# A hybrid attention, RWKV and expert layer on one core: three more row buffers for the first gathers, and a scheduling priority for block 0

## The chip, the core and the metric

The kernel runs on one core of one Trainium2 chip. The engines named below are TensorE (PE, with its weight loads as PEld), VectorE (DVE), ScalarE (ACT), GpSimd (POOL) and SyncE (SP, which here only issues DMAs). The metric is the device time of one execution in microseconds. The kernel before took a median of 1790.33 us in 3 runs (1789.28 to 1791.99).

## The reference

One layer on 512 tokens of width 1024, in float32: a norm, one input projection, two groups of heads beside each other (8 latent-attention heads, 8 RWKV-7 heads), an output projection, and a retrieval over 16,384 single-neuron experts. Cut to what matters here:

```python
x = x + concat(mla_group(p_a), rwkv7_group(p_b)) @ w_o
h = rms_norm(x)                                   # 128 tokens a block, 4 blocks
s = einsum('thpd,hpnd->thpn', h @ w_pq, sub_keys)
s1, i1 = top_k(s[:, :, 0], 16); s2, i2 = top_k(s[:, :, 1], 16)
top_s, pos = top_k(s1[..., :, None] + s2[..., None, :], 16)
idx = take(i1 * 128 + i2, pos)                    # 8 heads x 16 experts a token
gate = softmax(top_s)
act = gelu(einsum('thkd,td->thk', expert_u[idx], h))
x = x + einsum('thk,thkd->td', gate * act, expert_v[idx])
```

Each token needs 128 rows of `expert_u` and 128 rows of `expert_v`, each row 1024 floats.

## The kernel before

The 512 tokens are 4 blocks of 128. The front part runs as five "lanes" of generators that a planner at the end of `layer_kernel` (from L1178) interleaves: F (norm and RWKV input projections), R (RWKV chunk products), M (latent attention), S (RWKV scan) and B (`back`: output projection, norm, retrieval, routing). B runs for block 0, then for blocks 1 and 2 together, then for block 3. I write M(2) for lane M of block 2, and so on.

Within one lane of one block the steps depend on each other. R's products (`products`, L660) are eight 64-column matmuls by 64-row halves for each level of a block inverse, masked on DVE at L674 and copied on ACT at L681; they stand in a `tc.high_priority(offset=URGENT)` block. M ends in four transposes at L518 and copies to the tile `yT` at L520. `back` begins with `out_proj` (L784 matmuls, L788 adds), then `retrieve` (L840, L847), `top16` on DVE (L819 to L827), and `route` (L854 to L959). For blocks 0 and 3 `route` ends in `idx` (L952), the row numbers of the experts.

Experts are applied in two ways. Blocks 1 and 2 (`DENSE`) go through `dense()`: for each of 128 groups of 128 experts, `up(e)` multiplies with the transposed table (L1095, or split into three products at L1109) and `down(e)` with `expert_v` (L1130, or split at L1141). The splits are made on ACT (L1055) and DVE (L1056: tiles `xl`, `ul`, `t`). `gate_half` (L1035) builds the gates. Blocks 0 and 3 (`GATHERED`) go through `experts()`: for each of the 128 experts of a token, POOL issues an indirect DMA that fetches one row per token into a tile `ga` (L970), and DVE either takes the product with the hidden state (L980, a row of `expert_u`) or adds the row to the accumulator (L983, a row of `expert_v`). Rows of u come in four groups of 32; from the second group on, each u row is followed by a v row of the group before. In all there are 512 gathers, 256 for a block. The tiles `ga` rotate through 4 buffers (`GA`): a gather can be issued only when the DVE instruction that read the fourth one back is done.

The program is recorded through a scheduling layer. It assigns each instruction a place in its engine's queue by a priority (by default the order in which it was recorded) and by its own estimate of when inputs and buffers are ready; `high_priority(offset=4000)` moves the instructions recorded in it 4000 places ahead. What comes out is a fixed order on each engine, and each engine then runs its queue strictly in that order. `experts()` is recorded after `dense()`, so its gathers have the lowest priority, and fill in from the time when `idx` is known. The pools of the early stages (`early`, L102) are closed before `dense()`, which reuses their space.

Of the kernel before, what the change touches and what calls it, by code (L numbers as in the profile page):

```python
# [2 lines left out]

# [5 lines left out]
F32 = mybir.dt.float32  # L9
# [9 lines left out]
P = 128  # L19
D = 1024  # L20
# [8 lines left out]
LNX_EPS = 64e-5  # L29
TOPK = 16  # L30
URGENT = 4000
NEG = -3.0e38
MASKED = -1.0e30
LD = -0.5 * math.exp(-0.5)
# [31 lines left out]
GATHERED = (0, 3)  # L66
DENSE = (1, 2)
EARLY = 1
GROUP, GA = 32, 4


HALF, SUB, GBUFS = 64, 16, 5
FIRST, AHEAD, KEPT = 12, 16, 12
# [14 lines left out]
def layer_kernel(ctx: ExitStack, tc: tile.TileContext, x, pos, cvec, rvec, w_mla, w_rwkv, w_uq, w_ukv, lora, g2,  # L88
# [12 lines left out]
    psums[2] = ctx.enter_context(tc.tile_pool(name="psm", bufs=1, space=PSUM))  # L101
    early = ctx.enter_context(ExitStack())  # L102
    psa = early.enter_context(tc.tile_pool(name="psa", bufs=1, space=PSUM))
    pre = early.enter_context(tc.tile_pool(name="pre", bufs=1))
    wa = early.enter_context(tc.tile_pool(name="wa", bufs=1))
    for n in (1, 4):
# [747 lines left out]
    def route(b, tv, ti):  # L854
# [103 lines left out]
        for j, dst in enumerate(slots):  # L958
            act(dst[:, o:o + P], p[:, j * P:(j + 1) * P], AF.Copy)  # L959

    def experts(b, idx, gate):
        acc = gb([P, D], "acc")
        nc.sync.dma_start(acc, x2d[b])
        h2 = gb([P, D], "h2")
        nc.sync.dma_start(h2, h2r[b])
        dots = gb([P, H * TOPK], "dots")

        def row_of(table, j):
            t = gb([P, D], "ga", GA)
            G.indirect_dma_start(out=t, out_offset=None, in_=table,  # L970
                                 in_offset=bass.IndirectOffsetOnAxis(ap=idx[:, j:j + 1], axis=0))
            return t

        ng = H * TOPK // GROUP
        for g in range(ng + 1):
            for i in range(GROUP):
                if g < ng:
                    j = g * GROUP + i
                    u = row_of(expert_u, j)
                    V.scalar_tensor_tensor(u, u, 1.0, h2, op0=OP.mult, op1=OP.mult, accum_out=dots[:, j:j + 1])  # L980
                if g:
                    j = (g - 1) * GROUP + i
                    V.scalar_tensor_tensor(acc, row_of(expert_v, j), dots[:, j:j + 1], acc, op0=OP.mult, op1=OP.add)  # L983
            if g < ng:
                sl = slice(g * GROUP, (g + 1) * GROUP)
                act(dots[:, sl], dots[:, sl], AF.Gelu)
                V.tensor_tensor(dots[:, sl], dots[:, sl], gate[:, sl], op=OP.mult)
        nc.sync.dma_start(out[b * P:(b + 1) * P, :], acc)

    state = {"carry": None}  # L990
    hTs, yTs, parts, routed = {}, {}, {}, {}
# [197 lines left out]
    while any(lanes):  # L1189
        best = None  # L1190
        for i, todo in enumerate(lanes):
            if not todo:
                continue
            t = at[i]
            if running[i] is None:
                deps = [d for b in todo[0][1] for d in after[todo[0][0]](b) if d[1] >= 0]
                if any(d not in done for d in deps):
                    continue
                t = max([t] + [done[d] for d in deps])
            if best is None or t < best[0]:  # L1200
                best = (t, i)
        t, i = best
        n, bs = lanes[i][0]
        fn, count, cost = stages[n]
        if running[i] is None:
            running[i] = fn(bs) if n == "B" else fn(*bs)
            at[i] = t
        lane[0] = LANE[n]
        try:
            next(running[i])  # L1210
            at[i] += cost / count
        except StopIteration:
            for b in bs:
                done[n, b] = at[i]
            lanes[i].pop(0)
            running[i] = None
    early.close()
    dense()
    for b in GATHERED:
        experts(b, *routed[b])  # L1220


def pack(inputs):
# [55 lines left out]
```

## Time and profile before

| | before |
|---|---|
| median of 3 runs | 1790.33 us |
| the profiled execution | 1786.83 us |
| its span, first to last instruction | 1784.9 us |
| PE busy | 1622.3 us (91%) |
| DVE busy | 1352.8 us (76%) |
| ACT busy | 907.3 us (51%) |
| POOL busy | 723.1 us (41%) |
| data moved by the indirect DMAs | 268.47 MB of 520.84 MB |

The busy time of an engine is what its instructions took, added up without overlap; it is an average over stages that have different limits. The profile gives the same numbers for any stretch of the span, and with them the clock granted to TensorE and what the DMA engines moved. "Waited for" lines name who ended an idle stretch of an engine.

### The profile page before, as it was taken

The page shows a single profiled execution, that of the slowest core. Times are in us where ns is not written, and L with a number is a line of the kernel's source. Part 1 is how long each engine was busy: PE and PEld are TensorE (multiplying, and loading weights), DVE is VectorE, ACT ScalarE, POOL GpSimd, SP SyncE. Part 2 cuts the span into 40 slices and gives each one's busy share as a digit, 9 for nine tenths or more (in the row PEclk, how much of TensorE's full clock was granted, in tenths as well). Part 3 has the DMA queues.
Part 4 walks back from the last instruction along what each step waited for, and adds up shares of the span by engine and source line. Part 5 has one row for each costly group of instructions (what it writes and reads, how often), then busy time and mean ns, then how long its engine had stood idle before and what let it go on. Part 6 is the DMA issues. An engine that isn't in the chain of part 4 may idle for free. (4 is left out here: it accounts for less than half of the span.)

```text
span 1784.9 us, 31084 instructions
## 1 busy us (share of the span) xinstructions
PE 1622.3 (91%) x11143; PEld 1363.3 (76%) x11143; DVE 1352.8 (76%) x3010; ACT 907.3 (51%) x2421; POOL 723.1 (41%) x560
## 2 busy tenths in 40 slices
PE   7999998998879995789997799999989889999998
PEld 6896898877665784667995478888867778888876
DVE  3422446667775698987889789999878799999895
ACT  5645635444422622257766234444777735444444
POOL 1001100447664433555445343544555554447430
PEclk9999997995769998998998999999989999999999
DMA  8545643898789998889997799999889889999985
GB/s 276 187 139 191 237 163 111 322 313 268 262 272 329 318 313 305 287 297 331 376 328 244 284 363 355 330 348 340 313 318 324 310 306 355 373 340 333 354 280 177
DMA packets 154875, 520.84 MB, mean 292 GB/s; under 512 B 17313, under 2 KB 24097, under 8 KB 154721
## 3 DMA queue, kind: packets, MB, share of 16 engines
q0 software_dynamic: 73728, 268.47, 43.1%
q1 hardware_dynamic: 80992, 250.39, 39.3%
q8 instruction: 88, 1.44, 0.3%
q14 instruction: 67, 0.54, 0.1%
HBM read 508.96 MB, written 9.83 MB: 291 GB/s over the span
## 5 line engine op out<-in xcount | busy, mean ns | idle before, releaser
L970 POOL DMA_INDIRECT ga<-in_expert_v_dram,idx x256 | 359.0, 1402 | 366.7 <-DVE acc L983 260.9
L970 POOL DMA_INDIRECT ga<-in_expert_u_dram,idx x256 | 311.9, 1218 | 337.7 <-DVE ga L980 234.2
L983 DVE SCALAR_TENSOR_TENSOR acc<-ga,dots,acc 128x1024 f32<-128x1024 f32 x256 | 327.6, 1280 | 63.7 <-DMA ga<-in_expert_v_dram,idx 60.8
L980 DVE SCALAR_TENSOR_TENSOR ga<-ga,h 128x1024 f32<-128x1024 f32 x256 | 311.6, 1219 | 65.0 <-DMA ga<-in_expert_u_dram,idx 62.1
L1141 PE MATMUL po<-xh,t 128*128 128x512 f32 x880 | 305.2, 406 | 11.7 <-DVE t L1056 5.6
L1109 PE MATMUL ps<-dh,ul 128*128 128x256 f32 x664 | 192.7, 290 | 10.6 <-DVE ul L1056 10.0
L1055 ACT ACTIVATE xh<-v 128x512 fp32r<-128x512 f32 x220 | 136.4, 627 | 121.5 <-PE po L1141 99.7
L1109 PE MATMUL ps<-dh,uh 128*128 128x256 f32 x664 | 189.7, 286 | 6.7 <-ACT uh L1055 5.2
L1141 PEld LDWEIGHTS po<-xh,t 128*128 128x128 f32 x880 | 160.9, 192 | 44.4 <-DVE t L1056 6.8
L1141 PE MATMUL po<-xl,t 128*128 128x512 f32 x440 | 179.2, 408 | 11.1 <-DVE xl L1056 10.4
L1109 PE MATMUL ps<-dl,uh 128*128 128x256 f32 x664 | 188.7, 284 | 0.0
L1095 PE MATMUL ps<-t,u 128*128 128x256 f32 x720 | 172.5, 392 | 12.8 <-DMA u<-in_expert_ut_dram 11.1
L1056 DVE TENSOR_TENSOR xl<-v,xh 128x512 fp32r<-128x512 f32 x220 | 149.6, 688 | 36.6 <-ACT xh L1055 34.1
L1095 PEld LDWEIGHTS ps<-t,u 128*128 128x128 f32 x720 | 138.6, 197 | 36.8 <-issue 6.6
L1031 ACT ACTIVATE A<-iotap,slots 128x128 f32<-128x128 f32 x512 | 156.2, 394 | 0.0
L1035 PEld LDWEIGHTS ps<-B,A 128*128 128x128 f32 x1024 | 128.8, 200 | 23.2 <-ACT A L1032 11.9
L1109 PEld LDWEIGHTS ps<-dh,ul 128*128 128x128 f32 x664 | 127.3, 192 | 21.8 <-DVE ul L1056 16.5
L1055 ACT ACTIVATE uh<-u 128x512 fp32r<-128x512 f32 x166 | 99.7, 626 | 86.3 <-PE ps L1109 67.6
L1109 PEld LDWEIGHTS ps<-dh,uh 128*128 128x128 f32 x664 | 127.4, 192 | 16.7 <-ACT uh L1055 8.0
L1035 PE MATMUL ps<-B,A 128*128 128x64 f32 x1024 | 128.5, 281 | 10.6 <-ACT A L1032 9.4
L1109 PEld LDWEIGHTS ps<-dl,uh 128*128 128x128 f32 x664 | 127.3, 192 | 3.0 <-issue 0.2
L840 PE MATMUL ps<-h2T,wst 128*128 128x128 f32 (+1 forms) x768 | 123.5, 315 | 1.6 <-DMA wst<-in_w_pq_dram 1.6
(391 smaller groups left out, 2845.7 us busy)
## 6 DMA issues: line engine op xcount, KB each, us to landing
u<-in_expert_ut_dram SPq DMA_DIRECT2D x128, 512.0 KB
v<-in_expert_v_dram SPq DMA_DIRECT2D x128, 512.0 KB
wst<-in_w_rwkv_dram SPq DMA_DIRECT2D x56, 512.0 KB
wst<-in_w_pq_dram SPq DMA_DIRECT2D x48, 512.0 KB
wst<-in_w_o_dram SPq DMA_DIRECT2D x24, 512.0 KB
wst<-in_w_mla_dram SPq DMA_DIRECT2D x16, 336.0 KB
t<-in_x_dram SPq DMA_DIRECT2D x8, 512.0 KB
wst<-in_w_ukv_dram SPq DMA_DIRECT2D x16, 256.0 KB
```

Source lines behind the costliest of these rows:

```text
L840: mm(p[:, :nb * P], w[:, kc, :], h2T[:, kc, :], start=kc == 0, stop=kc == KC - 1)
L970: G.indirect_dma_start(out=t, out_offset=None, in_=table, in_offset=bass.IndirectOffsetOnAxis(ap=idx[:, j:j + 1], axis=0))
L980: V.scalar_tensor_tensor(u, u, 1.0, h2, op0=OP.mult, op1=OP.mult, accum_out=dots[:, j:j + 1])
L983: V.scalar_tensor_tensor(acc, row_of(expert_v, j), dots[:, j:j + 1], acc, op0=OP.mult, op1=OP.add)
L1031: act(A[:, j, :], iotap, AF.Abs, scale=-1.0, bias=i2T[:, t0 + j:t0 + j + 1])
L1035: mm(p[:, j * HALF:(j + 1) * HALF], A[:, j, :], B[:, j, :], start=True, stop=True)
L1055: act(hi, t, AF.Copy)
L1056: V.tensor_tensor(lo, t, hi, op=OP.subtract)
L1095: mm(p, u[:, kc, :], hd[kc // 2][:, kc % 2, :], start=kc == 0, stop=kc == KC - 1)
L1109: mm(p, a[:, k, :], h[:, kc, :], start=kc + i == 0, stop=kc == KC - 1 and i == 2)
L1141: mm(po[i][n], ww[:, i * P:(i + 1) * P], vv, start=e + k == 0, stop=e == P - 1 and k == 2)
```

## The change

Three things are changed. A new pool `gx` with three tiles of the size of `ga` is opened among the early pools. `experts()` becomes a generator that yields after each pair of rows, and its first 96 steps for block 0 (the u rows of groups 0 to 2 and the v rows of groups 0 and 1, 96 + 64 = 160 gathers) are now recorded before the early pools are closed and before `dense()`. In those 160, gathers take their tiles in turns of seven, four from `ga` and three from `gx`; after them only `ga` is used. And every step of `back` for block 0 is recorded inside `high_priority(offset=URGENT)`.

```diff
+HURRIED = "B"
+GX, WIDE = 3, 96
...
+    gx = early.enter_context(tc.tile_pool(name="gx", bufs=1))
...
+    n_rows, spare = [0], [True]
+
     def experts(b, idx, gate):
...
         def row_of(table, j):
-            t = gb([P, D], "ga", GA)
+            turn = n_rows[0] % (GA + GX)
+            n_rows[0] += 1
+            if spare[0] and turn >= GA:
+                t = gx.tile([P, D], F32, tag="gx", name=f"gx{n_rows[0]}", bufs=GX)
+            else:
+                t = gb([P, D], "ga", GA)
...
+                if i < GROUP - 1:
+                    yield
             if g < ng:
...
+            yield
         nc.sync.dma_start(out[b * P:(b + 1) * P, :], acc)
...
-            next(running[i])
+
+            with tc.high_priority(offset=URGENT) if bs == (0,) and n in HURRIED else nullcontext():
+                next(running[i])
...
+    rows = [experts(b, *routed[b]) for b in GATHERED]
+    for _ in range(WIDE):
+        next(rows[0])
+    spare[0] = False
     early.close()
     dense()
-    for b in GATHERED:
-        experts(b, *routed[b])
+    for r in rows:
+        for _ in r:
+            pass
```

The scheduling layer makes a new order of all queues from this. Line numbers of the kernel after are a few higher: the gather L970 is L981 there, L917 is L921, L1056 is L1070. Three places show what moved.

On POOL, at the first gathers of block 0, the kernel before has these rows (`onr` is a step of M(1), `gnr` of S(1), the MEMSETs belong to R(2)):

```order
L567 TENSOR_TENSOR rn_3776<-rn_3776,mhalf 128x8
L303 TENSOR_TENSOR onr_3169<-onv_3167,mhalf 128x8
L970 DMA ga_15350<-in_expert_u_dram,idx_3068 128x1024
L970 DMA ga_15353<-in_expert_u_dram,idx_3068 128x1024
L970 DMA ga_15356<-in_expert_u_dram,idx_3068 128x1024
L613 MEMSET t_4004 64x512
L970 DMA ga_15359<-in_expert_u_dram,idx_3068 128x1024
L970 DMA ga_15362<-in_expert_u_dram,idx_3068 128x1024
L303 TENSOR_TENSOR gnr_3889<-gnv_3887,mhalf 128x8
```

and the kernel after has these:

```order
L571 TENSOR_TENSOR rn_3779<-rn_3779,mhalf 128x8
L617 MEMSET t_4007 64x512
L307 TENSOR_TENSOR gnr_3892<-gnv_3890,mhalf 128x8
L617 MEMSET t_4006 64x512
L307 TENSOR_TENSOR onr_3172<-onv_3170,mhalf 128x8
L981 DMA ga_7189<-in_expert_u_dram,idx_3071 128x1024
L981 DMA ga_7192<-in_expert_u_dram,idx_3071 128x1024
L981 DMA ga_7195<-in_expert_u_dram,idx_3071 128x1024
L981 DMA ga_7198<-in_expert_u_dram,idx_3071 128x1024
L981 DMA gx_7201<-in_expert_u_dram,idx_3071 128x1024
L981 DMA gx_7204<-in_expert_u_dram,idx_3071 128x1024
L981 DMA gx_7207<-in_expert_u_dram,idx_3071 128x1024
```

Both MEMSETs and `gnr`, which stood among the gathers, now stand ahead of the first one; then seven gathers follow without a break, the last three into `gx`.

On DVE, in the last part of block 0's `route` (`t` is its ring of partial sums, `pi` and `bf` its ranks), the kernel before has:

```order
L917 SCALAR_TENSOR_TENSOR t_2896<-pi_2800,dl_2779 128x128
L503 RECIPROCAL rz_3104<-z_2266 128x8
L917 SCALAR_TENSOR_TENSOR t_2896<-pi_2800,dl_2779 128x128 x8
L917 SCALAR_TENSOR_TENSOR t_2896<-bf_2914,dl_2779 128x128 x14
L334 COPY carry_3477<-hT_3418 128x8
L917 SCALAR_TENSOR_TENSOR t_2896<-bf_2914,dl_2779 128x128 x2
```

and the kernel after has, in the same part:

```order
L921 SCALAR_TENSOR_TENSOR t_2899<-pi_2803,dl_2782 128x128
L507 RECIPROCAL rz_3107<-z_2269 128x8
L773 TENSOR_TENSOR t_3947<-t_3947,ga_1476 128x512
L604 TENSOR_SCALAR sg_3992<-sg_3992 128x128
L921 SCALAR_TENSOR_TENSOR t_2899<-pi_2803,dl_2782 128x128 x7
L778 TENSOR_TENSOR yT_1673<-t_3947,ps_3955 128x512
L921 SCALAR_TENSOR_TENSOR t_2899<-pi_2803,dl_2782 128x128
L622 TENSOR_TENSOR pm_2093<-ps_4022,pm_2093 128x512
L921 SCALAR_TENSOR_TENSOR t_2899<-bf_2917,dl_2782 128x128 x7
L633 TENSOR_TENSOR t_4039<-ps_4040,mmask 128x4x128
```

Steps of S(1) (L773, L778) and of R(2) (L622, L633), which came after `route` before, now stand between its partial sums. Up to `idx` of block 0 the kernel after has 1650 PE instructions (before 1594), 499 on DVE (476) and 500 on ACT (471).

Late in `dense()`, around the groups 111 and 112, DVE's queue of the kernel before has (`xl` and `ul` are low halves of `v` and `u`, `acc` is block 3's accumulator, `q` and `t` are activations):

```order
L1056 TENSOR_TENSOR xl2121_14864<-v111_14857,xh2121_14863 128x512
L983 SCALAR_TENSOR_TENSOR acc2433_16127<-ga2687_16893,dots2435_16131,acc2433_16127 128x1024
L1126 TENSOR_TENSOR q2119_14855<-q2119_14855,G_7203 128x256
L1056 TENSOR_TENSOR ul2124_14887<-u127_14883,uh2124_14886 128x512
L1056 TENSOR_TENSOR ul2125_14903<-u127_14883,uh2125_14902 128x512
L983 SCALAR_TENSOR_TENSOR acc2433_16127<-ga2688_16896,dots2435_16131,acc2433_16127 128x1024
L1056 TENSOR_TENSOR xl2122_14874<-v111_14857,xh2122_14873 128x512
L1056 TENSOR_TENSOR t22138_15026<-wst2042_14106,t22138_15026 128x256
L1056 TENSOR_TENSOR xl2127_14926<-v112_14919,xh2127_14925 128x512
L983 SCALAR_TENSOR_TENSOR acc2433_16127<-ga2689_16899,dots2435_16131,acc2433_16127 128x1024
```

and the kernel after has at the same groups:

```order
L1070 TENSOR_TENSOR ul2219_15382<-u127_15378,uh2219_15381 128x512
L1070 TENSOR_TENSOR xl2216_15359<-v111_15352,xh2216_15358 128x512
L1070 TENSOR_TENSOR xl2217_15369<-v111_15352,xh2217_15368 128x512
L1070 TENSOR_TENSOR t22233_15521<-wst2137_14601,t22233_15521 128x256
L1070 TENSOR_TENSOR ul2220_15398<-u127_15378,uh2220_15397 128x512
L1140 TENSOR_TENSOR q2214_15350<-q2214_15350,G_7698 128x256
L1070 TENSOR_TENSOR xl2222_15421<-v112_15414,xh2222_15420 128x512
L1070 TENSOR_TENSOR xl2223_15431<-v112_15414,xh2223_15430 128x512
```

The additions of gathered rows are gone from this place: in the kernel after the last gather stands earlier in the queue.

## Rows read from the trace of the kernel before

**Rows 1.** Page, part 1: busy us (share of the span) and instructions.
```profile
PE 1622.3 (91%) x11143; PEld 1363.3 (76%) x11143; DVE 1352.8 (76%) x3010; ACT 907.3 (51%) x2421; POOL 723.1 (41%) x560
```
**Rows 2.** Windows by stage: us, busy of each engine, clock, DMA share, GB/s.
```profile
core 0: us, PE busy (x) PEld busy (x) DVE busy (x) ACT busy (x) POOL busy (x), PEclk, DMA share, GB/s
318.00:408.00 90.00, 85.98 (x816) 70.35 (x815) 63.61 (x132) 41.14 (x146) 44.08 (x39) 0.96 0.90 323
408.00:535.00 127.00, 100.78 (x773) 86.59 (x773) 97.74 (x144) 49.83 (x148) 83.32 (x65) 0.64 0.81 269
535.00:626.00 91.00, 85.12 (x620) 60.47 (x619) 55.22 (x102) 42.29 (x137) 43.70 (x37) 1.00 0.91 324
626.00:700.00 74.00, 66.96 (x396) 59.48 (x396) 64.55 (x235) 22.63 (x68) 29.58 (x28) 0.99 0.91 317
700.00:760.00 60.00, 36.88 (x182) 30.53 (x183) 58.20 (x275) 13.53 (x37) 30.36 (x24) 0.81 0.81 281
...
944.00:1004.00 60.00, 46.76 (x192) 31.13 (x192) 54.55 (x183) 24.43 (x58) 25.62 (x15) 0.86 0.71 232
...
1650.00:1737.00 87.00, 81.14 (x489) 70.26 (x487) 80.71 (x111) 40.36 (x83) 34.67 (x25) 1.00 0.89 317
```
**Rows 3.** Source L952: first and last start of `idx`.
```profile
L952 ACT ACTIVATE idx<-ps x2: 278/278/278, 318.2 to 1004.4; 128x128 int32<-128x128 f32 x2
```
**Rows 4.** Source L627: R's matmuls, min/median/max ns, first and last start.
```profile
L627 PE MATMUL ps<-t,t x128: 272/272/373, 62.5 to 486.9; 64*128 64x128 f32 x128
```
**Rows 5.** Who waited on DVE, 318 to 408 us: total us, times, longest.
```profile
DVE ga L980 <- DMA ga<-in_expert_u_dram,idx: 9.1, 8, 2.5
```
**Rows 6.** The same, 408 to 535 us.
```profile
DVE acc L983 <- DMA ga<-in_expert_v_dram,idx: 11.1, 13, 3.0
DVE ga L980 <- DMA ga<-in_expert_u_dram,idx: 10.0, 14, 1.8
```
**Rows 7.** The same, 535 to 626 us.
```profile
DVE acc L983 <- DMA ga<-in_expert_v_dram,idx: 14.7, 8, 5.0
DVE ga L980 <- DMA ga<-in_expert_u_dram,idx: 5.1, 5, 2.1
```
**Rows 8.** Who waited on PE, 408 to 535 us, the longest.
```profile
PE ps L666 <- DVE t L674: 12.1, 4, 4.4
```
**Rows 9.** Windows of source L970, the gather issues: POOL busy (count).
```profile
408.00:535.00 127.00, 75.37 (x60) 0.64 0.81 269
```
**Rows 10.** Windows of source L983, v rows on DVE: busy (count).
```profile
408.00:535.00 127.00, 35.27 (x28) 0.64 0.81 269
944.00:1004.00 60.00, 19.14 (x15) 0.86 0.71 232
1650.00:1737.00 87.00, 35.87 (x28) 1.00 0.89 317
```
**Rows 11.** Windows of source L980, u rows, two records each.
```profile
318.00:408.00 90.00, 35.48 (x58) 0.96 0.90 323
```
**Rows 12.** Page, part 3: the queue of the indirect DMAs, packets, MB.
```profile
q0 software_dynamic: 73728, 268.47, 43.1%
```
**Rows 13.** Windows: the 50 us in which the DMAs moved most.
```profile
850.00:900.00 50.00, 50.00 (x382) 48.12 (x380) 42.90 (x110) 36.59 (x98) 21.21 (x18) 1.00 0.99 372
```
**Rows 14.** Who waited on PE, 626 to 720 us, the longest.
```profile
PE ps L518 <- ACT t L513: 19.2, 1, 19.2
```
**Rows 15.** Who waited on PE, 1650 to 1737 us, all.
```profile
PE ps L1109 <- ACT uh L1055: 2.0, 2, 1.0
PE po L1141 <- ACT t L1055: 1.6, 2, 0.8
PE ps L1109 <- DVE ul L1056: 1.5, 4, 0.7
PE po L1141 <- ACT xh L1055: 0.5, 1, 0.5
```
**Rows 16.** The chain that ended last, its end: start, us, what.
```profile
1737.32 37.45 PE po L1141 x159
```

More of the change, by code (lines that the diff above doesn't have):

```diff
@@ L1 @@
 import math
-from contextlib import ExitStack
+from contextlib import ExitStack, nullcontext
 import concourse.bass as bass
```

## The prediction, made before the changed kernel ran

> **What bounds the kernel now.** I read the busy times first, then the windows by stage, then the waits of the two engines that stand out, and last the order of the queues before and after. The busy times say little: PE 91%, DVE 76% [rows 1]. The windows say where each limit lies [rows 2]. From 408 to 535 us DVE is busy 97.74 of 127 us, PE runs at a granted clock of 0.64, and the DMAs are at 0.81. DVE's other time there is mostly waiting for gathered rows, 11.1 + 10.0 = 21.1 us [rows 6]; together 118.8 of 127 us, so DVE sets that stage. What PE waits for longest is DVE's masks of the R products, 12.1 us [rows 8]: in the queue they stand behind gathers. From 535 to 626 us PE is at 85.12 of 91 us at full clock and DVE has room. From 626 us on DVE is nearly always busy: 64.55 of 74, 58.20 of 60, 54.55 of 60 us. In 1650 to 1737 us both are near full (PE 81.14, DVE 80.71 of 87), and the end is PE alone: 37.45 us of `down` products without a break [rows 16].
>
> **The change, part by part.** Sums go by the profiled execution, 1786.83 us (a span of 1784.9 and 1.93 around it); the median of the runs is 3.50 us above it.
>
> The priority. It should bring `idx` of block 0, now at 318.2 us [rows 3], forward. The order says otherwise: ahead of `idx` there stand 56 more PE instructions, 23 more on DVE, 29 on ACT. Most of the 56 are R and S products; at the 0.272 us of a 128-column one [rows 4] that is up to 56 x 0.272 = 15 us, and nothing at the lower end, where other lanes' waits hide them. They are not added work: they leave the place where they stood. PE is busy 85.98 of 90 us from 318 on [rows 2], so it works through them in either order. I cost the edit at 0 on the path and note that the first gather starts some 12 us later, about 330 us. If that cover fails, 15 us.
>
> The buffers, first effect: fewer waits. In 408 to 535 us POOL issues 60 gathers, one each 127 / 60 = 2.12 us [rows 9]. With 4 buffers a buffer goes round in 4 x 2.12 = 8.5 us; of that the issue is 75.37 / 60 = 1.26 us and the DVE instruction that frees it 35.27 / 28 = 1.26 us [rows 10], so 6.0 us are landing and standing in queues. Seven buffers with the same round give one each 1.21 us, past the next limits: DVE at 1.26, POOL at 1.26, and the DMAs at 268.47 MB / 512 = 0.524 MB [rows 12] over the 372 GB/s of the fastest 50 us [rows 13] = 1.41 us. So the row wait of 21.1 us in the DVE-bound stage could go wholly (-21.1), or not at all (0) if it comes from load on the DMAs. I take half, -10: the stage's DMA share of 0.81 leaves room, but not for a doubled rate.
>
> A page speaks against this term. The trace has 6.0 us between issue and use in this stage. The Trainium skill, "DMA: Bandwidth & Descriptors", section "Anatomy of one DMA — SWDGE (gpsimd) path", gives for one such DMA about 2.0 us plus its bytes over 436 GB/s. By that, 3.2 us (an estimate from that page) would be all a row needs, four buffers would go round in 5.7 us, a row each 1.4 us, and three more would have nothing to hide; the measured 2.12 us does not agree, and it decides here.
>
> The buffers, second effect: more rows early. Counted in DVE's queue (and before, counted off in the trace's DVE instructions to get the time), when 653 instructions of other kinds are through, at 626 us before, 119 gathers have been used before and 142 after. These 23 are 23 x 1.25 = 29 us of DVE, between the 35.48 / 29 = 1.22 us of a u row [rows 11] and the 1.26 us above. By the order they stand late in the stretch, after the 607th other instruction, which is 535 to 626 us. There DVE has 91 - 55.22 = 35.8 us idle, 19.8 us of it waiting for rows [rows 2, 7]. If those waits shrink, the 29 us fit: 0. If none shrinks, 16.0 us are free and 13 are late; at worst none is free, +29. The DMAs say the same: 324 GB/s x 91 us + 23 x 0.524 MB = 41.5 MB, at 372 GB/s 112 us, +21. I take +8, nearer the low end, because the extra buffers let these rows be fetched ahead of the stage, up to three of them at a time.
>
> The later stages. From that point to the 16th split of a `v` half (1062 us) the queue uses 153 gathers before and 150 after: 3 x 1.25 = -4 us in a stage that DVE mostly sets, 0 where it does not; I take -3. Block 0 is done before block 3's `idx`, where before 15 rows (19.14 us, rows of 944 to 1004 us [rows 10]) were mixed into its routing; but block 3's rows then begin sooner, and at the 16th split it is 292 against 272, which leaves the same load. From there to about 1650 us each queue has the same instructions with the difference of 20 gathers kept: 0.
>
> The end. Of the 28 rows used after 1650 us [rows 10] 8 are left, 25 us less DVE work. PE idles only 87 - 81.14 = 5.9 us there [rows 2], on ACT and DVE in shares of 2.0, 1.6, 1.5, 0.5 us [rows 15], and the last 37.45 us hold no row at all. So between 0 and -6; I take -3, since most of these waits name ACT.
>
> Sum: 0 - 10 + 8 - 3 - 3 = -8 us: 1778.8 for the profiled execution, 1782 against the median.
>
> **The rivals.**
>
> Full DMAs: the row waits come from load, not from the number of buffers. For it: shares of 0.90 and 0.91 on both sides of the stage [rows 2]; against it: 0.81 within. Then the first term is 0 and the 29 us are split as now, about +8, with -6 from the last two: 1787 to 1792, no change that can be told.
>
> Slower: rows in front of M(2). M is the lane that ends last: PE stands 19.2 us at 700 us, waiting for M(3) to finish [rows 14]. In the order after, the end of M(2) (L520) has 101 gathers and 612 other DVE instructions ahead of it, where it had 83 and 602, and 217 more PE instructions, most of them R(3) products. If DVE has no idle time to give, those 18 rows delay M(2) by 18 x 1.25 = 23 us, hence the output projection of blocks 1 and 2, M(3) and that PE stand. It decides once row waits stay above about 50.0 - 29 = 21 us of the 9.1 + 21.1 + 19.8 = 50.0 us in 318 to 626 us [rows 5 to 7]. Price +23 less 6 later: about 1807.
>
> Faster by the clock: if DVE no longer starves PE in 408 to 535 us, PE's 100.78 us at 0.64 could run at full clock. 21.1 us of waits gone and some 10 us of matmul time with them: 1786.83 - 21 - 10 + 8 - 6 + 3.5, about 1761. Against it: the R products depend on each other level by level, and the PE idles between them in either order.
>
> **How the numbers follow.** Forecast case (1775 to 1790): 0.43, of which 0.33 are faster by over 0.2% (3.6 us, about what measuring this kernel can tell from no change) and 0.10 within it. Full DMAs: 0.13, of which 0.09 within and 0.04 faster. M(2) delayed: 0.32, all but 0.01 slower by over 0.2%. Clock: 0.12, faster. Together faster 0.49, same 0.20, slower 0.31. The range for 8 in 10 reaches from the clock case to the M(2) case, 1760 to 1808; the likeliest case alone has 1775 to 1790.
>
> **What would show it.** Block 0's `idx` between 318 and 333 us. DVE's waits for row data in the stages up to 626 us: under 25 us confirms the first two terms, over 40 the slower rival. Gathers one each 1.5 to 1.9 us while `gx` is in use. The first L840 of blocks 1 and 2 near 600 us, and the end of M(3) near 720 us: both more than 15 us later would make the forecast wrong. The last row of block 3 used about 50 us before the end of `down` instead of beside it. If `idx` of block 3 came earlier than 1004 us but the end did not, the later stages are set by DVE's total, as assumed.

## The result: 1.3% slower

The changed kernel takes 1814.88 us (median of 4 runs, 1808.49 to 1819.32), the kernel before beside it 1789.80 us (4 runs, 1782.06 to 1791.99): a ratio of 1.013, 95% interval 1.0091 to 1.0169. The forecast was 1782 with a range of 1760 to 1808, so it was wrong in sign, and the median lies 7 us beyond the range. The profiled execution took 1817.47 us (span 1815.7), 30.6 us more than that of before.

The page's busy times of the changed kernel, to set beside [rows 1]:

```profile
PE 1640.9 (90%) x11143; PEld 1378.9 (76%) x11143; DVE 1353.8 (75%) x3010; ACT 913.2 (50%) x2423; POOL 723.3 (40%) x560
```

The same 11143 matrix products (the PE instructions of all lanes in the trace, called products below) were busy for 18.6 us longer (the mean granted clock of the run is 0.930 instead of 0.942), so PE's idle time grew by only 30.8 - 18.6 = 12.2 us. DVE's busy time is the same within 1 us. The windows of the changed kernel by the stages of [rows 2]:

```profile
core 0: us, PE busy (x) PEld busy (x) DVE busy (x) ACT busy (x) POOL busy (x), PEclk, DMA share, GB/s
318.00:408.00 90.00, 87.31 (x910) 72.72 (x911) 60.85 (x150) 38.82 (x130) 41.55 (x36) 0.97 0.75 277
408.00:535.00 127.00, 112.12 (x957) 92.99 (x955) 109.30 (x168) 52.35 (x154) 88.56 (x70) 0.73 0.89 312
535.00:626.00 91.00, 66.63 (x271) 42.16 (x270) 57.89 (x94) 34.08 (x121) 58.68 (x46) 0.78 0.91 338
626.00:700.00 74.00, 63.97 (x330) 55.09 (x331) 63.37 (x191) 23.08 (x63) 38.04 (x33) 0.92 0.96 345
700.00:760.00 60.00, 36.47 (x208) 31.96 (x206) 53.90 (x235) 16.53 (x46) 25.28 (x23) 0.77 0.82 286
944.00:1004.00 60.00, 56.17 (x373) 49.48 (x371) 47.72 (x217) 52.44 (x135) 4.35 (x1) 0.94 0.44 150
1650.00:1737.00 87.00, 86.81 (x551) 78.08 (x550) 76.43 (x110) 45.02 (x88) 41.88 (x19) 1.00 0.87 309
```

The stage on which the forecast rested did improve: from 408 to 535 us PE was busy 112.12 us instead of 100.78, DVE 109.30 instead of 97.74. The loss shows in the next one: from 535 to 626 us PE ran 271 products where it had run 620, at a granted clock of 0.78 instead of 1.00, while DVE did no more than before. DVE's waits for rows there, the answer to [rows 5 to 7] (first three windows, in order):

```profile
DVE gx L991 <- DMA gx<-in_expert_u_dram,idx: 3.8, 3, 2.2
DVE ga L991 <- DMA ga<-in_expert_u_dram,idx: 1.8, 2, 1.3
...
DVE gx L991 <- DMA gx<-in_expert_u_dram,idx: 2.4, 2, 1.3
DVE acc L994 <- DMA ga<-in_expert_v_dram,idx: 2.0, 1, 2.0
DVE acc L994 <- DMA gx<-in_expert_v_dram,idx: 0.6, 1, 0.6
DVE ga L991 <- DMA ga<-in_expert_u_dram,idx: 0.2, 1, 0.2
...
DVE ga L991 <- DMA ga<-in_expert_u_dram,idx: 3.3, 1, 3.3
```

They fell from 50.0 to 14.1 us, more than forecast, and the kernel is slower all the same. So what was to be won was won, and something else was lost. Where, the mixings M (lane M, one for each block) show. Their ends are the last products of L518 (L522 in the changed kernel), last start in the line of each:

```profile
L518 PE MATMUL ps<-ident,t x16: 272/273/473, 139.1 to 723.4; 128*128 128x128 f32 x16
```

```profile
L522 PE MATMUL ps<-ident,t x16: 272/273/473, 140.3 to 759.7; 128*128 128x128 f32 x16
```

M(3), which opens `dense()`, ends 36 us later. In windows cut at the ends of M(0), M(1), M(2) and M(3), first before, then after:

```profile
142.00:329.00 187.00, 181.03 (x1660) 153.43 (x1659) 85.75 (x368) 100.17 (x334) 17.63 (x16) 0.95 0.56 188
329.00:518.00 189.00, 163.15 (x1401) 139.14 (x1400) 142.37 (x245) 79.85 (x252) 112.22 (x89) 0.75 0.85 291
518.00:724.00 206.00, 171.57 (x1143) 134.43 (x1142) 154.59 (x477) 71.85 (x224) 93.16 (x81) 0.93 0.88 308
```

```profile
144.00:344.00 200.00, 189.54 (x1706) 158.71 (x1705) 90.97 (x377) 102.77 (x340) 19.12 (x17) 0.96 0.50 166
344.00:559.00 215.00, 190.99 (x1785) 160.04 (x1785) 166.51 (x277) 89.78 (x270) 137.36 (x111) 0.80 0.88 317
559.00:760.00 201.00, 149.59 (x703) 114.37 (x701) 162.51 (x495) 63.66 (x202) 108.64 (x91) 0.85 0.93 339
```

From M(0) to M(3) PE runs nearly the same number of products (4204 and 4194), but 384 more of them stand beside M(2) and 440 fewer beside M(3). Most of the shift is lane R's: the products of L666 (L670 in the changed kernel) in the windows of M(2) and M(3), before and then after, are

```profile
329.00:518.00 189.00, 43.86 (x624) 41.41 (x624) 0.75 0.85 291
518.00:724.00 206.00, 19.25 (x336) 17.96 (x336) 0.93 0.88 308
```

```profile
344.00:559.00 215.00, 63.80 (x960) 59.05 (x960) 0.80 0.88 317
559.00:760.00 201.00, 0.00 (x0) 0.00 (x0) 0.85 0.93 339
```

M(2) takes 26 us longer, and PE is busy in 28 us more of it; M(3), with 703 products instead of 1143, still takes 201 us, and PE is idle in 51 of them (34 before). The whole loss has arisen by the end of M(3). Up to there PE runs the same products in both kernels, busy 15.3 us longer with them and idle 20.7 us longer:

```profile
0.00:724.00 724.00, 644.39 (x5502) 537.95 (x5503) 432.22 (x1284) 332.11 (x1063) 233.80 (x204) 0.90 0.73 249
0.00:760.00 760.00, 659.66 (x5501) 544.61 (x5501) 469.45 (x1343) 336.76 (x1065) 275.90 (x235) 0.89 0.74 258
```

From M(3) to the end of the span it is 1061 us before and 1056 after: the rest gave back 5.

### The profile page after: what moved, and what is told of

Same layout as the page of the kernel before. It is cut to its first block, busy times and chain, and to the rows that moved or that the text cites. A ratio compares the mean times of both kernels' runs of the same rounds, so it can differ in the third digit from the quotient of the medians.

```text
span 1815.7 us, 31106 instructions
## 1 busy us (share of the span) xinstructions
PE 1640.9 (90%) x11143; PEld 1378.9 (76%) x11143; DVE 1353.8 (75%) x3010; ACT 913.2 (50%) x2423; POOL 723.3 (40%) x560
## 3 DMA queue, kind: packets, MB, share of 16 engines
q0 software_dynamic: 73728, 268.47, 41.2%
## 4 chain that ended last, share of the span: by engine, by line
PE 52%; issue 15%; DVE 13%; DMA 11%; POOL 6%; ACT 3%; SPq 0%; POOLq 0%; DVEq 0%; ACTq 0%
PE po L1155 12%; PE ps L1123 10%; PE ps L354 6%; POOL ga L981 5%; DMA ga<-in_expert_v_dram,idx 5%; PE ps L844 4%; PE ps L670 4%; DVE acc L994 3%; DMA ga<-in_expert_u_dram,idx 3%; DVE ga L991 2%; PE ps L1049 2%; PE ps L1109 1%; PE ps L788 1%; PE ps L365 1%; DMA u<-in_expert_ut_dram 1%
## 5 line engine op out<-in xcount | busy, mean ns | idle before, releaser
L981 POOL DMA_INDIRECT ga<-in_expert_v_dram,idx x228 | 314.1, 1378 | 301.5 <-DVE acc L994 204.9
L981 POOL DMA_INDIRECT ga<-in_expert_u_dram,idx x216 | 274.3, 1270 | 325.1 <-DVE ga L991 177.0
L994 DVE SCALAR_TENSOR_TENSOR acc<-ga,dots,acc 128x1024 f32<-128x1024 f32 x228 | 291.4, 1278 | 45.2 <-DMA ga<-in_expert_v_dram,idx 42.7
L991 DVE SCALAR_TENSOR_TENSOR ga<-ga,h 128x1024 f32<-128x1024 f32 x216 | 262.6, 1219 | 52.9 <-DMA ga<-in_expert_u_dram,idx 49.1
L1070 DVE TENSOR_TENSOR xl<-v,xh 128x512 fp32r<-128x512 f32 x220 | 148.8, 687 | 39.8 <-ACT xh L1069 37.3
L844 PE MATMUL ps<-h2T,wst 128*128 128x128 f32 (+1 forms) x768 | 127.9, 322 | 10.9 <-issue 8.7
```

The lines of the kernel that those rows point to most:

```text
L844: mm(p[:, :nb * P], w[:, kc, :], h2T[:, kc, :], start=kc == 0, stop=kc == KC - 1)
L981: G.indirect_dma_start(out=t, out_offset=None, in_=table, in_offset=bass.IndirectOffsetOnAxis(ap=idx[:, j:j + 1], axis=0))
L1070: V.tensor_tensor(lo, t, hi, op=OP.subtract)
```

## The experiments

Six theories were put against each other, as the runs called for them. A: the early rows cost DVE time. A': they fill the DMA engines, and weights come late. B: the priority is guilty. C: the new order is guilty (that of the scheduling layer, called the planner in the expectations), by what it puts beside M(2) instead of M(3). D: the sum of all engines' work decides, in whatever order. E: the rows' work on all engines taken together. All numbers in one table: the ratio to the kernel before in runs on the same chip with its 95% interval; then from the profile the lengths in us (and products) from M(1) to M(2) and from M(2) to M(3), the end of M(3), and the end of the last row's DVE instruction. The lengths are of one profiled execution each. The time of one kernel varies between its runs (the changed kernel from 1808.49 to 1819.32 us, the kernel before from 1773.29 to 1799.41 us in one set), so a difference of a few us between two lengths tells nothing.

| kernel | ratio | M(2) | M(3) | M(3) ends | last row |
|---|---|---|---|---|---|
| before | 1 | 189 (1401) | 206 (1143) | 724 | 1736 |
| after | 1.013 (1.0091 to 1.0169) | 215 (1785) | 201 (703) | 760 | 1713 |
| rows_alone | 1.0056 (1.0023 to 1.0089) | 199 (1602) | 203 (944) | 731 | 1699 |
| priority_alone | 0.9975 (0.9936 to 1.0013) | 168 (1437) | 189 (1051) | 698 | 1747 |
| half_columns | 1.0108 (1.0032 to 1.0184) | 198 (1830) | 198 (664) | 737 | 1669 |
| half_bytes | 1.0033 (1.0003 to 1.0063) | 166 (1360) | 205 (1133) | 714 | 1630 |
| same_order_half_bytes | 1.0232 (1.0171 to 1.0293) | 220 (1829) | 195 (662) | 769 | 1725 |
| others_behind | 1.0079 (1.0042 to 1.0116) | 201 (1597) | 193 (869) | 737 | 1718 |
| rows_after_mixing | 1.0374 (1.03 to 1.0447) | 180 (1483) | 191 (1006) | 715 | 1674 |
| mixing_first | 1.0168 (1.0117 to 1.0218) | 141 (1357) | 178 (1567) | 577 | 1817 |
| mixing_and_hurry | 1.0212 (1.0167 to 1.0256) | 145 (1303) | 188 (1288) | 592 | 1785 |
| mixing_and_rows | 1.0092 (1.0061 to 1.0124) | 143 (1327) | 234 (1793) | 640 | 1777 |
| one_buffer_fewer | 1.013 (1.0082 to 1.0178) | 200 (1393) | 216 (1150) | 749 | 1792 |
| hurry_and_first_mixing | 0.9979 (0.995 to 1.0008) | 196 (1533) | 200 (1286) | 704 | 1762 |
| rows_cheap_after | 1.0076 (1.0048 to 1.0105) | 210 (1829) | 174 (632) | 735 | 1702 |
| rows_cheap_before | 0.9739 (0.9693 to 0.9786) | 175 (1503) | 185 (1059) | 695 | 1688 |

### Each half of the change by itself

```diff
-HURRIED = "B"
+HURRIED = ""
```

> The three extra buffers and the early use of 96 of block 0's gathers, without the priority. Theory A (the rows that the extra buffers let in early stand on VectorE in front of the last blocks' mixing and retrieval, and what is lost there does not come back): 1805 to 1820 us, with the end of the last block's mixing near 755 us as in the changed kernel. Theory A' (the same stretch, but lost to full DMA engines and not to VectorE): the same time. Theory B (the priority for block 0 is what delays the other blocks): 1780 to 1792, with that end near 725 us.

```diff
-    n_rows, spare = [0], [True]
+    n_rows, spare = [0], [False]
```

(and no pool `gx`, and `WIDE = 0`, so that all rows are recorded after `dense()` as in the kernel before.)

> The priority alone, rows as in the kernel before. A and A': 1780 to 1795 us, block 0's indices between 330 and 342 us, the end of the last block's mixing within 10 us of the 723 us of before. B: 1803 to 1818, and that end later than 740 us.

1797.2 and 1784.45 us, where the kernel before had 1788.99. B falls: the priority alone costs nothing that can be told, and its M(3) ends 26 us earlier. (From there to the end of the span it is 1084 us instead of 1061.) But A and A' are not borne out either: the rows alone cost 0.56%, less than half of the loss, with M(3) at 731 and not at 755. The two parts together cost more than their sum, and what goes with that is the number of products beside M(2): 1437 and 1602 apart, 1785 together (1401 before).

### DVE time or DMA bytes

```diff
+                    w = D // 2 if b == 0 else D
-                    V.scalar_tensor_tensor(u, u, 1.0, h2, ...
+                    V.scalar_tensor_tensor(u[:, :w], u[:, :w], 1.0, h2[:, :w], ...
...                  # the same width for the additions to acc
```

> The changed kernel, but VectorE multiplies and adds only the first 512 of the 1024 columns of block 0's rows (the other half is left out); the gathers fetch the same bytes. A: a row costs VectorE about half, so that some 47 rows between 590 and 690 us cost some 25 us less there, and the last block's mixing ends before 738 us instead of 760; 1780 to 1795 us in all. A': that end stays later than 750 us, and the time above 1800. B: as A'.

```diff
+            w = D // 2 if b == 0 else D
-            G.indirect_dma_start(out=t, out_offset=None, in_=table,
+            G.indirect_dma_start(out=t[:, :w], out_offset=None, in_=table if b else table.rearrange("e (a w) -> (e a) w", a=2),
...                  # and each use of a row in two operations of w columns
```

> The changed kernel, but each of block 0's gathers fetches rows of 512 columns instead of 1024 (other data, half the bytes), and VectorE uses them twice, in two operations of 512 columns, so that its work on a row stays. A: VectorE has as much to do, the last block's mixing ends between 750 and 770 us, and the time stays above 1800. A': with the DMA engines no longer full between 590 and 690 us that end comes before 740 us, and the time falls to 1780 to 1795.

half_columns ended M(3) at 737, as A said, but took 1812.51 us, as A' said: DVE time moved the end of M(3), 23 us, and not the end of the kernel (from M(3) on 1072 us instead of 1056; why was not followed). half_bytes took 1794.33 us with M(3) at 714, which looked like A'. It was not clean: with smaller DMAs the planner had made another order, with 1360 products beside M(2). The next kernel has half the bytes in the order of the changed kernel.

```diff
+            if b == 0:
+                act(idx[64:], p[64:, :P], AF.Copy, scale=0.0, bias=1e6)
...
-                                 in_offset=bass.IndirectOffsetOnAxis(ap=idx[:, j:j + 1], axis=0))
+                                 in_offset=..., bounds_check=table.shape[0] - 1, oob_is_err=False)
...                  # row buffers and half of h2 are cleared on DVE beforehand
```

> The changed kernel in nearly its own order of instructions, but each of block 0's gathers fetches rows for 64 of the 128 partitions (the other 64 get an index past the table and are skipped, their rows are left out), so half the bytes. In half_bytes, which also had half the bytes, the order of TensorE had changed with it: block 2's mixing ended after 2377 of TensorE's matrix instructions instead of 2594, as in the kernel before. Theory A' (the DMA engines are full and the weights come late): the last block's mixing ends before 735 us, as with half_bytes (714), and the time is 1785 to 1800. Theory C (the planner, that gives the rows' DMAs time too, puts some 200 instructions of the scan and of other lanes ahead of block 2's mixing; the mixing of a block is a chain that takes about 200 us even when little stands beside it, so what was put ahead of it is not won back): the order is that of the changed kernel, the last mixing ends at 745 to 762 us, and the time is 1803 to 1818.

1831.49 us. Its windows between the ends of M(1), M(2) and M(3):

```profile
354.00:574.00 220.00, 195.60 (x1829) 166.65 (x1825) 175.75 (x292) 93.78 (x289) 154.51 (x118) 0.79 0.59 198
574.00:769.00 195.00, 147.57 (x662) 112.22 (x661) 157.50 (x490) 59.07 (x183) 113.73 (x88) 0.83 0.68 233
```

The DMA share is 0.59 and 0.68 instead of 0.88 and 0.93, and both links (the stretch from one M's end to the next) are about as long as in the changed kernel, 220 and 195 us. A' falls. C's own numbers were missed too: M(3) ends at 769 us (762 at most was expected), and the time is 13 us above C's range. M(0) already ends 10 us later here, after row buffers are cleared on DVE; the rest of the added time was not followed.

### The order by itself

```diff
-            with tc.high_priority(offset=URGENT) if bs == (0,) and n in HURRIED else nullcontext():
+            late = URGENT if bs == (0,) and n in HURRIED else -URGENT if n in "RS" and bs >= (2,) else 0
+            with tc.high_priority(offset=late) if late else nullcontext():
```

> The changed kernel with the recurrence and scan of blocks 2 and 3 at a priority 4000 lower. The rows come at the same points (99 of them before block 2's mixing ends, 101 in the changed kernel), but that mixing ends after 2513 TensorE instructions instead of 2594. C: about 80 instructions at some 0.23 us each, so that the last mixing ends 12 to 25 us earlier, at 735 to 748 us, and the time falls to 1792 to 1805. A': the same bytes in the same stretch, no gain: 752 us or later, above 1808.

1804.08 us, M(3) at 737: both as C said. With the rows kept and 188 products fewer beside M(2), M(2) is 14 us shorter and M(3) no longer, and from M(3) on it is 1056 us as in the changed kernel. The ratio falls from 1.013 to 1.0079; the two intervals overlap, so that the gain in time is not shown by itself. The last pair makes block 0's rows nearly free in either order (diff of the one made from the changed kernel; the other has the same lines in the kernel before):

```diff
+            if b == 0:
+                act(idx[32:64], p[32:64, :P], AF.Copy, scale=0.0, bias=1e6)
+                act(idx[64:], p[64:, :P], AF.Copy, scale=0.0, bias=1e6)
...
+                    w = 64 if b == 0 else D
+                    V.scalar_tensor_tensor(u[:, :w], u[:, :w], 1.0, h2[:, :w], ...
...                  # the bounds check and the clearing as above, the same width for acc
```

> The changed kernel with block 0's rows nearly free: 96 of the 128 partitions skip their rows (a quarter of the bytes) and VectorE multiplies and adds 64 of the 1024 columns (the rest is left out). The order stays: block 2's mixing ends after 2605 TensorE instructions (2594 in the changed kernel). C (order alone): from the end of block 1's mixing to the end of block 3's 385 to 415 us (changed kernel 416), and 25 us or more above rows_cheap_before. Theory E (the rows' own work on VectorE, GpSimd and the DMA engines taken together makes the mixing long): under 365 us, and within 12 us of rows_cheap_before. The time itself falls in both, since VectorE is freed of block 0's rows.

> The kernel before with block 0's rows nearly free in the same way. Block 2's mixing ends after 2417 TensorE instructions (2377 before). From the end of block 1's mixing to that of block 3's (before: 395 us): by C 340 to 375 us and at least 25 us under rows_cheap_after; by E within 12 us of it.

1804.46 and 1745.43 us: 59 us apart with rows that cost next to nothing. The windows from the end of M(1) on, rows_cheap_before and then rows_cheap_after:

```profile
335.00:510.00 175.00, 160.35 (x1503) 132.39 (x1503) 64.30 (x241) 81.88 (x256) 90.60 (x86) 0.89 0.46 141
510.00:695.00 185.00, 165.90 (x1059) 131.18 (x1057) 82.04 (x497) 71.37 (x220) 74.88 (x73) 0.94 0.56 177
```

```profile
351.00:561.00 210.00, 194.17 (x1829) 165.05 (x1827) 65.52 (x253) 91.16 (x271) 95.78 (x93) 0.81 0.41 124
561.00:735.00 174.00, 140.70 (x632) 107.97 (x632) 61.48 (x371) 58.94 (x196) 93.28 (x92) 0.88 0.62 197
```

M(2) and M(3) take 360 us in the order of before and 384 in the order after; the bounds set for C were missed by 1 us in each case (384 instead of 385, 24 instead of 25), those for E (under 365, within 12) by 19 and by 12. With full rows the two take 395 and 416. So the new order, with all that the change moved in it, costs 21 us with full rows and 24 with cheap ones, and the rows cost 35 us in the order of before and 32 in the changed one: what a row costs is not what differs between the kernels. PE's idle time says the same: 60.3 and 75.4 us with full rows, 33.7 and 49.1 with cheap ones, 15 more by the order in each pair. A, A' and E fall as the cause of the loss in the links, and C is left; that it is the products beside M(2), and nothing else in the new order, rests on the counts and on others_behind. The two profiles of the pair are 60 us apart: 24 in the two links, 16 ahead of them (M(1) is 13 us longer), and 20 after M(3) (1047 and 1067 us to the end of the span), which were not followed.

### Tries at a better kernel, and the limits of C

The first took one extra buffer, from row 85 on, and recorded all of block 0's rows ahead of `dense()`; the next three gave the mixings of all blocks the priority (the first two of them without the extra buffers and the early rows; the second with block 0's priority and R and S of blocks 2 and 3 behind, the third with the extra buffers too).

```diff
+            if spare[0] and turn >= GA and n_rows[0] > 85:      # rows_after_mixing, GX, WIDE = 1, 128
...
+            late = URGENT if n == "M" else 0                    # mixing_first
```

> The priority as in the changed kernel, but one extra buffer instead of three, used from row 85 on, and all of block 0's gathers recorded ahead of the dense part: few rows beside block 2's mixing (it ends after 2452 instructions and 74 rows), more rows later. A' and C both: the last mixing ends at 695 to 712 us. Whether the earlier end is kept is what it tells: with block 3's rows done sooner than in priority_alone, 1765 to 1782 us if rows were what held that kernel's end; 1782 to 1795 if rows beside the dense part cost as much there as beside the mixing.

> The kernel before with the mixing of all four blocks at a priority 4000 higher, nothing else. It ends after 486, 1046, 1788 and 2653 of TensorE's matrix instructions (before: 702, 1634, 2377 and 2982), the last scan after 3078 (2830), and block 0's indices come after 1865 (1594). C (the four mixings are a chain of some 190 us each that nothing can shorten, so what stands ahead of its links decides): the first ends some 30 us earlier, the last before 700 us instead of 724, and the dense part begins 15 to 30 us earlier; since block 0's rows begin later (209 of them instead of 254 used by block 3's indices), part of it goes again: 1765 to 1785 us. Rival D (the work of all engines up to there decides, and not the chain): the last mixing earlier but the scan as much later, 1785 to 1800.

> As mixing_first, with the changed kernel's priority for block 0 as well and the recurrence and scan of blocks 2 and 3 at a priority 4000 lower: the mixings end after 486, 1057, 1805 and 2490 instructions, the last scan after 3078, block 0's indices after 1734. C: the last mixing before 690 us; rows earlier than in mixing_first (239 used by block 3's indices), so 1755 to 1780. D: 1785 to 1800.

> As mixing_and_hurry, with the three extra row buffers too (the changed kernel with the mixings first). The last mixing ends after 2762 instructions, the last scan after 3046; 107 rows by the end of the third... by the end of the last mixing. C: with the mixing ahead of the scan the extra rows no longer stretch the last link; the dense part begins within 10 us of mixing_and_hurry's, and the time is 1755 to 1785, 30 us or more under the changed kernel. D: as the changed kernel, above 1800.

1857.74, 1822.04, 1826.5 and 1808.49 us: no forecast of a time held but D's "above 1800" for the last, and all four are slower than the kernel before. In rows_after_mixing M(3) ends at 715 us, 3 us outside what was expected, but then the kernel loses where `dense()` opens. That the rows recorded ahead hold it up was not shown: PE's longest waits from 714 to 900 us name the DMAs of `u` and of `w_pq` (15.7 and 15.5 us) and ACT at L801 (12.4). PE from 760 to 900 us, where it was 129.96 us busy before:

```profile
760.00:900.00 140.00, 92.99 (x472) 74.50 (x470) 107.46 (x262) 30.25 (x84) 75.16 (x62) 0.78 0.92 349
```

mixing_first refutes one half of C as it was put: a mixing is no chain of 190 us that nothing can shorten, M(2) took 141 and M(3) 178. M(3) ended 147 us earlier, and the last PE work came 13 us earlier (1765 instead of 1778). But block 0's indices came at 422 us instead of 318, and now the rows end the kernel. The last two windows:

```profile
1690.00:1767.00 77.00, 64.76 (x260) 44.14 (x260) 67.40 (x100) 27.58 (x53) 41.81 (x31) 0.98 0.90 320
1767.00:1821.00 54.00, 0.00 (x0) 0.00 (x0) 33.77 (x28) 0.00 (x0) 28.74 (x23) 0.50 0.76 261
```

PE has nothing to do in the last 54 us, in which 26 rows are still added. In the other two the indices come at 387 us, the last row is used at 1785 and 1777 and the last product ends at 1810; what set their ends was not followed. mixing_and_rows refutes C's forecast for it: its M(3) ends 48 us later than that of mixing_and_hurry (within 10 was expected), with 1793 products beside M(3) instead of 1288, and still it is the faster of the two. So a later end of M(3) is not by itself a slower kernel; priority_alone and half_columns say the same from the other side.

The last two kernels, one with three row buffers instead of four for block 0's first rows (`GA - 1`), one with the priority and M(0) hurried as well (`URGENT if n == "M" and bs[0] in (0,)`):

> The other way: the kernel before with three row buffers instead of four for the first 96 steps of block 0's rows (the fourth is used from then on), no priority. Block 2's mixing ends after 2361 TensorE instructions (before 2377, with more buffers 2404, 2425 and 2481) and 75 rows (83). C: the last mixing between 705 and 725 us, rows later (232 instead of 254 by block 3's indices) but still under the end of the dense part: 1778 to 1792 us. If what costs is each row that is early, by its own time on VectorE and the DMA engines, 8 rows fewer there give 5 to 12 us: the last mixing before 715, 1775 to 1785 us.

> The priority alone, and the mixing of block 0 at the same priority: the mixings end after 486, 1430, 2292 and 2982 TensorE instructions (priority_alone: 702, 1664, 2409, 2982), the last scan after 2974, rows a little later (234 by block 3's indices, 238). C: links that begin earlier and fewer instructions ahead of block 2's: the last mixing at 675 to 697 us, 1768 to 1783 us in all unless the rows end it (last row later than 1760 us). D (the work of all engines up to there decides): last mixing near 698 as in priority_alone, 1780 to 1790 us.

1814.6 and 1786.06 us. one_buffer_fewer was expected at 1775 to 1792 by either theory and lost as much as the changed kernel, for the opposite reason: the order beside M(2) and M(3) is that of before (1393 and 1150 products), but DVE waits longer for rows. In the windows of [rows 5 to 7]:

```profile
DVE ga L989 <- DMA ga<-in_expert_u_dram,idx: 10.2, 7, 3.1
...
DVE ga L989 <- DMA ga<-in_expert_u_dram,idx: 17.5, 20, 2.4
DVE acc L992 <- DMA ga<-in_expert_v_dram,idx: 11.7, 8, 3.0
...
DVE ga L989 <- DMA ga<-in_expert_u_dram,idx: 14.2, 6, 5.5
DVE acc L992 <- DMA ga<-in_expert_v_dram,idx: 11.4, 11, 2.5
```

65.0 us, against 50.0 with four buffers and 14.1 with seven. Over the whole of M(2) and M(3), for the kernel before, one_buffer_fewer and the changed kernel:

```profile
DVE acc L983 <- DMA ga<-in_expert_v_dram,idx: 29.2, 23, 5.0
DVE ga L980 <- DMA ga<-in_expert_u_dram,idx: 29.1, 31, 3.8
...
DVE ga L989 <- DMA ga<-in_expert_u_dram,idx: 50.3, 36, 5.5
DVE acc L992 <- DMA ga<-in_expert_v_dram,idx: 33.9, 24, 3.6
...
DVE ga L991 <- DMA ga<-in_expert_u_dram,idx: 10.4, 7, 4.1
DVE gx L991 <- DMA gx<-in_expert_u_dram,idx: 7.1, 6, 2.2
DVE acc L994 <- DMA ga<-in_expert_v_dram,idx: 3.4, 2, 2.0
DVE acc L994 <- DMA gx<-in_expert_v_dram,idx: 0.6, 1, 0.6
```

That is 58.3, 84.2 and 21.5 us: with one buffer fewer DVE waits 26 us longer, and M(3) ends 25 us later. So the buffers do matter as the forecast had it, but the way back does not hold: 37 us less waiting in the changed kernel goes with two links that are 21 us longer. hurry_and_first_mixing speaks for D and not for C: M(3) at 704 us (C 675 to 697, D near 698) and a time within D's 1780 to 1790. D is not ruled out there. Of the kernels that compute everything only hurry_and_first_mixing and priority_alone have ratios below 1, and both intervals include 1: no version was shown to beat the kernel before.

## Why the prediction was wrong

**The priority at 0 on the path.** Block 0's indices came at 339.9 instead of 318.2 us (forecast about 330, and between 318 and 333 as a sign):

```profile
L956 ACT ACTIVATE idx<-ps x2: 267/268/268, 339.9 to 999.1; 128x128 int32<-128x128 f32 x2
```

M(1) took 200 us instead of 187, and 197 in priority_alone, 187 in rows_alone. The 56 instructions were seen and their price, up to 15 us, was named; it was set to 0 because "they are not added work". Up to the indices PE was busy 16 us longer, 314.99 us instead of 298.87. For the edit by itself the 0 came out at the end: in priority_alone M(2) and M(3) together are 38 us shorter. In the changed kernel M(1)'s 13 us were not made good.

The step that failed is this pricing of what only moves, here and above all for the 217 PE instructions that the new order puts ahead of the end of M(2): the sum has no term for them. What the runs showed in its place is M(2) 26 us longer and M(3) only 5 shorter, 21 us in all, and 24 us with rows that are nearly free. Products that move were not free where the next link waited behind them, and little came back where they had stood.

**Fewer row waits, -10.** Right about the waits: of the 21.1 us in 408 to 535 us 15.9 went, and 36 of the 50.0 us in 318 to 626. The time did not follow: M(2) and M(3) together are 21 us longer, and rows_alone, which has the buffers without the priority, is 0.56% slower than the kernel before. The load on the DMAs was no obstacle to the shorter waits. The Trainium skill, "DMA: Bandwidth & Descriptors", section "Anatomy of one DMA — SWDGE (gpsimd) path", was weighed there with an estimated 3.2 us for a row; that more buffers took away most of the waits does not agree with it, and a row took longer than that to land beside this kernel's other traffic. The median from issue to landing is 6.8 us for rows of u in priority_alone, with four buffers, and 7.3 us in rows_alone:

```profile
ga<-in_expert_u_dram,idx POOLq DMA_INDIRECT x216, 7.3
```

**23 more rows early, +8.** This put the risk on the wrong quantity. Rows that are nearly free leave the loss of the two links as it was (21 and 24 us), so the extra rows' own work was not its cause.

**The slower rival, rows in front of M(2).** It had the place and nearly the time (1807), and a wrong mechanism. It named 217 more PE instructions before the end of M(2) (in the trace 440 more products, 4801 instead of 4361) and then priced only 18 rows of DVE time; that its time came so near is luck. Its condition, row waits that stay above 21 us, was not met (14.1), and the loss came all the same. What it lacked is the products' own time: M(2) 26 us longer, M(3) only 5 shorter with PE idle for 17 us more of it and slower, and M(1) 13 longer, of which priority_alone shows 10. With M(0) 2 us later that makes the 36 us.

**The later stages, -3, and the end, -3.** From M(3) on -5 was measured, so about right in sum, but not as told. Block 0's rows are done before block 3's indices, as said, and POOL then stands still:

```profile
POOL ga L981 <- ACT idx L956: 55.9, 1, 55.9
```

From 944 to 1004 us it issues one gather, with the DMAs at a share of 0.44. At the end PE is busy 86.81 of 87 us (the same from 1681 to 1768 us, as far from the end as the window of before) where it was 81.14, so that its idle time there, 5.9 us, is all but gone, as the lower bound of -6 had it; the last row is used at 1713 instead of 1736 us. So the end gave about what both terms were to give together, and the later stages nothing.

**Full DMAs; the clock.** same_order_half_bytes speaks against the first. The clock case did not come: 0.64 became 0.73 from 408 to 535 us as hoped, but 1.00 became 0.78 in the next stage, and the mean of the run fell from 0.942 to 0.930.

**The signs set beforehand.** M(3) later than 735 us and the first L840 of blocks 1 and 2 later than 615 (they came at 760 and 630) were to make the forecast wrong, and did. Row waits under 25 us were to confirm the first two terms: they were 14.1 us, and the terms did not hold, so this sign could not tell. The last row of block 3 was to be used about 50 us before the end of `down`; it was 95 us. Block 3's indices came 5 us earlier and the end did not, which was to show that DVE's total sets the later stages; from 760 to 1650 us PE was busy for 92% of the time and DVE for 86%, and no run tested it. Gathers were to come one each 1.5 to 1.9 us with `gx` in use; from 408 to 535 us there are 65, one each 1.95 us, just outside (POOL busy with them, [rows 9] before):

```profile
408.00:535.00 127.00, 81.34 (x65) 0.73 0.89 312
```

## What to carry to other kernels

When buffers or priorities change under a planner, compare how many products of other lanes stand beside each link of the longest chain, and price those that moved: here they cost where they arrived (M(2), 26 us) and gave little back where they left (M(3), 5 us). More buffers did take away the waits they were meant for, and that said nothing of the end. Nor does the end of the longest chain say all: M(3) came 26 us earlier in priority_alone, and no gain in time can be told. An ablation that changes the planner's costs changes the order too (half_bytes); change the data instead (same_order_half_bytes).

## What was not expected of the hardware

Of the 30.8 us of longer span, 18.6 are the same products taking longer: from 535 to 626 us, with PE busy 66.63 of 91 us, the granted clock was 0.78 (a mean of its two levels, 1.2 and 2.4 GHz), where it had been 1.00 with 85.12 us busy [rows 2]. It was low until 552.7 us and fell three times more, at 580.0, 607.3 and 614.1 us, each time near the end of a wait of PE of 2.9, 3.0 and 3.8 us for DVE or ACT. So the stage lost time to its waits and to the clock. The busy share alone does not tell the clock: from 408 to 535 us PE was busy for 112.12 of 127 us at 0.73. And an indirect DMA whose indices lie past the bound for 64 of 128 partitions moved half as much: all indirect DMAs of same_order_half_bytes together moved 201.42 MB instead of 268.47, which is half for block 0's 256 gathers (198 instead of 317 GB/s beside M(2), other traffic included). DVE's row waits did not get shorter by it, 26.2 us in M(2) and M(3) instead of 21.5.
